# Moving the residual to the token layout: turned in place and sent in 32 transfers, in place of 160

## The chip, the core and the metric

The kernel runs on one core of a Trainium2 chip. The metric is device time in microseconds for one execution: the median of several runs. Five engines work side by side, each on an instruction queue of its own that it takes strictly in order: TensorE (PE, the matrix products), VectorE (DVE), ScalarE (ACT), GpSimd (POOL) and SyncE (SP). SP computes nothing; in this kernel it issues nearly all transfers (DMAs), which 16 DMA engines then carry out.

## What is computed

One decoder layer on 256 tokens of width 2048, with 16 meta tokens put ahead of them. Cut to what matters:

```python
h = concat(meta, x)                              # 272 tokens x 2048
...                                              # sparse attention and causal pooling
mix = concat(attn_out, pool_out) @ w_o
h = layer_norm(ALPHA * h + mix, ln1_g, ln1_b)
f = conv_gated_ffn(h, w_up, conv_w, conv_b, w_down)   # up to 2 x 5632, causal conv of width 3, gelu(a) * g, down
h = layer_norm(ALPHA * h + f, ln2_g, ln2_b)
return h[:, N_META:]
```

The change touches the term ALPHA * h of the last sum, the residual of the feed-forward part.

## The kernel before, in words

All matrix products are float32 work done in three passes: each operand is split into a high part and a low part (tiles with a middle dimension of 2), and high x high, high x low and low x high are added in PSUM. So every weight tile goes the same way. SP loads 1 MB into a raw tile (`wraw`, line 87), ACT writes the high half in two pieces (line 90), DVE subtracts and writes the low half in two pieces (line 91, tile `whl`), and TensorE uses it. There are three `wraw` and three `whl` buffers. `weights()` asks for the tile two ahead of the one in use, so SP's queue holds the loads in the order of use, each waiting for a `wraw` buffer to come free, and whatever else SP issues stands between them.

Up to the first layer norm the data lie with channels on the partitions: `y` is [128 partitions, 16 blocks of 128 channels, 272 tokens]. `normalise` (lines 629 to 637) finishes the first layer norm block by block in `y` and writes the split copy `hp` that the feed-forward part multiplies. The feed-forward part runs over 44 blocks f of 128 hidden channels, in four parts of 16, 12, 12 and 4 (`PARTS`). Each f takes two weight tiles (the two halves of `w_up`), 96 matmuls, two convolutions (`conv`, lines 660 to 662: one ACT and two DVE instructions each) and a gate (lines 677 to 681). For f below 4 (`FOLDED`) the normalisation is folded into the product, so that TensorE can start before `normalise` is done; from f = 4 on the products use `hp`. After the blocks of a part come the down products of that part, in four column groups c of 512 output channels, and line 735 adds each result to `y2`.

`y2` is [128 tokens, 2 token halves, 2048 channels]: here tokens lie on the partitions. The normalised h, which the residual needs, lies in `y` with channels on the partitions. So it has to be moved to the other layout before line 735 adds the first down product to it. That is done in two steps:

- `turn_blocks(m)` (lines 641 to 644) has DVE transpose block m in squares of 32 x 32, after the gates of f = 4 to 7, four blocks each. Each block is written one place further down: block m into the place of block m - 1, and block 0 into a spare tile of the ring (`blocks`, shown as `turned` in the trace). Each DVE instruction covers 128 x 256 elements.
- `residual(c, a, b, i)` (lines 646 to 654) has SP send squares to their places: for source partitions 32a to 32a + 31 and 32 tokens, the squares of the four blocks of one column group c go to the 32 partitions of those tokens. For c = 1 to 3 that is one transfer of 16 KB (line 651). For c = 0 it is two, 12 KB from `y` (line 653) and 4 KB from the spare tile (line 654). Every contiguous piece is 32 elements, or 128 bytes. In all that makes 128 moves and 160 transfers.

The moves are listed by column group first (line 656). After the gate of each f from 5 on, ten of them are issued (lines 716 to 718), and ten more in each column group of the down products of part 0 (lines 731 and 732), until none is left. So line 735 of column group c waits only for the transfers of that group.

The kernel is written in a tile framework. It places the semaphores and lays out each engine's queue when the program is built. It follows the order of the source roughly, but may put an instruction that is ready by its own estimate ahead of one that is not. It spreads the transfers of a queue over a fixed set of semaphores, so an issue can also have to wait until an earlier transfer has landed.

Of the kernel before, what the change touches and what calls it, by code (L numbers as in the profile page):

```python
# [11 lines left out]
F32 = mybir.dt.float32  # L12
# [5 lines left out]
P = 128  # L18
D = 2048
NM = 16  # L20
S = 256
T = NM + S
# [13 lines left out]
FOLDED = 4  # L36
# [14 lines left out]
def tile_layer(ctx, tc, xt, w_first, w_proj, w_uk, w_uv, w_pool, w_o, w_up, w_down, cols, rows, rel_bias, onehot, out):  # L51
    nc = tc.nc
    sb = ctx.enter_context(tc.tile_pool(name="sb", bufs=1))
    wp = ctx.enter_context(tc.tile_pool(name="wp", bufs=3))
    ring = ctx.enter_context(tc.tile_pool(name="ring", bufs=24))
# [4 lines left out]
    def big():  # L60
        return pm.tile([P, 512], F32, tag="mm", name="mm")
# [34 lines left out]
    def emit(i):  # L96
        if i in ready:
            return
        if i == last:

            raw = wp.tile([P, 2048], F32, tag="wraw", name="wraw")
            nc.sync.dma_start(raw, stream[i])
            ready[i] = []
            for c in range(0, 2048, 256):
                hl = ring.tile([P, 2, 256], F32R, tag="act", name="whl_r", padded_shape=[P, 2, T])
                nc.scalar.activation(hl[:, 0, :], raw[:, c:c + 256], AF.Copy)
                nc.vector.tensor_tensor(hl[:, 1, :], raw[:, c:c + 256], hl[:, 0, :].bitcast(F32), op=ALU.subtract)
                ready[i].append(hl)
            return
        if i == spare:  # L110
            raw = wp.tile([P, 2048], F32, tag="wraw", name="wraw")
            hl = sb.tile([P, 2, 2048], F32R, tag="y", name="whl_y")
        else:
            raw, hl = weight_tiles()
        fetch(raw, hl, stream[i], slice(0, 2048))
        ready[i] = hl
# [6 lines left out]
    def weights(ahead=2):  # L123
        i = state["use"]
        state["use"] += 1
        prefetch(i + 1 + ahead)
        return ready.pop(i)
# [7 lines left out]
    def product(ps, hl, m, act, lo, hi, ks=range(KT), width=P, k0=0, k1=KT):  # L135

        for n in range(k0, k1):
            k = ks[n]
            wh, wl = hl[:, 0, k * width:k * width + m], hl[:, 1, k * width:k * width + m]
            ah, al = act[k][:, 0, lo:hi], act[k][:, 1, lo:hi]  # L140
            nc.tensor.matmul(ps, wh, ah, start=n == 0, stop=False)  # L141
            nc.tensor.matmul(ps, wh, al, start=False, stop=False)  # L142
            nc.tensor.matmul(ps, wl, ah, start=False, stop=n == KT - 1)  # L143
# [3 lines left out]
    for k0, k1 in [(k, k + 1) for k in range(9)] + [(9, 12), (12, 15), (15, 16)]:  # L147
# [7 lines left out]
        for k in range(k0, k1):  # L155
            xk, wk, c = raw[:, k % 3, :T], raw[:, k % 3, T:], slice(k % 6 * MF, k % 6 * MF + MF)
            a = ring.tile([P, 2, T], F32R, tag="act", name="xp")
# [184 lines left out]
    y = sb.tile([P, KT, T], F32, tag="y", name="x", padded_shape=[P, KT, T])  # L342
# [26 lines left out]
    src = score  # L369
    for r in range(TOPK // 8):  # L370
# [4 lines left out]
        src = work  # L375
# [228 lines left out]
    def deviation():  # L604
        ps = small()
        column_sums([s1], cuts, 0, ps)
        column_sums([s2], cuts, 1, ps)
        for i, (a, b) in enumerate(cuts):
            r = slice(0, b - a)
            nc.vector.tensor_scalar_mul(st[r, 0, i:i + 1], ps[r, 64 * i:64 * i + 1], 1.0 / D)  # L610
            nc.vector.tensor_scalar(st[r, 1, i:i + 1], ps[r, 64 * (3 + i):64 * (3 + i) + 1], 1.0 / D, EPS,
                                    op0=ALU.mult, op1=ALU.add)
        nc.vector.tensor_tensor(st[:, 2, :], st[:, 0, :], st[:, 0, :], op=ALU.mult)
        nc.vector.tensor_tensor(st[:, 1, :2], st[:, 1, :2], st[:, 2, :2], op=ALU.subtract)
        nc.vector.tensor_tensor(st[:2, 1, 2:], st[:2, 1, 2:], st[:2, 2, 2:], op=ALU.subtract)
        nc.gpsimd.tensor_tensor(st[:, 2, :], st[:, 1, :], half, op=ALU.pow)
        nc.vector.scalar_tensor_tensor(st[:, 3, :], st[:, 0, :], -1.0, st[:, 2, :], op0=ALU.mult, op1=ALU.mult)

    def deviation_rows():
        for j, dst in ((2, rs), (3, m2)):  # L620
            ps = small()
            spread(st[:, j, :], cuts, ps)
            nc.scalar.activation(dst, ps[:, :NQ], AF.Copy)


    y2 = fp.tile([P, 2, D], F32, name="y2", bufs=1)
# [9 lines left out]
        nc.vector.tensor_tensor(a[:, 1, :NQ], yd, a[:, 0, :NQ].bitcast(F32), op=ALU.subtract)  # L636
        h_parts.append(a)

    blocks = ring.tile([P, 2, T], F32, tag="act", name="turned0")

    def turn_blocks(m):

        dst = y[:, m - 1, NM:] if m else blocks[:, 0, NM:]
        nc.vector.transpose(dst, y[:, m, NM:])

    def residual(c, a, b, i):

        src, dst, t = slice(32 * a, 32 * a + 32), slice(32 * b, 32 * b + 32), NM + i * P + 32 * b
        to = y2[dst, i, 512 * c:512 * c + 512].rearrange("p (m d) -> p m d", d=P)[:, :, src]
        if c:  # L650
            nc.sync.dma_start(to, y[src, 4 * c - 1:4 * c + 3, t:t + 32])
        else:
            nc.sync.dma_start(to[:, 1:], y[src, :3, t:t + 32])
            nc.sync.dma_start(to[:, 0], blocks[src, 0, t:t + 32])  # L654

    moves = [(c, a, b, i) for c in range(4) for a in range(4) for b in range(4) for i in range(2)]

    def conv(j, half_, src):
        z = fp.tile([P, S], F32, name="z", tag=f"z{half_}")
# [16 lines left out]
    def gate(za, zg):  # L676
        nc.scalar.activation(za, za, AF.Gelu_apprx_tanh)
        nc.vector.tensor_tensor(za, za, zg, op=ALU.mult)
        a = fp.tile([P, 2, S], F32R, name="gp", tag="gp", bufs=18, padded_shape=[P, 2, NE])
        nc.scalar.activation(a[:, 0, :], za, AF.Copy)  # L680
        nc.vector.tensor_tensor(a[:, 1, :], za, a[:, 0, :].bitcast(F32), op=ALU.subtract)
        return a
# [3 lines left out]
    for part, n in enumerate(PARTS):  # L686
        gated = []
        for f in range(f0, f0 + n):
            if part == len(PARTS) - 1 and f - f0 in (0, 2):
                emit((last, spare)[(f - f0) // 2])  # L690
            both = []
            for half_ in range(2):
                hl = weights()
                ps = big()
                if f < FOLDED:
                    k = 0
                    if f + half_ == 0:
                        product(ps[:, :NE], hl, P, folded, 0, NE, k1=7)
                        deviation()
                        product(ps[:, :NE], hl, P, folded, 0, NE, k0=7, k1=14)  # L700
                        deviation_rows()
                        k = 14
                    product(ps[:, :NE], hl, P, folded, 0, NE, k0=k)
                    while len(h_parts) < min(KT, 3 * (2 * f + half_ + 1)):
                        normalise(len(h_parts))
                    both.append(ps)
                else:
                    product(ps[:, :NQ], hl, P, h_parts, 0, NQ)
                    both.append(conv(half_ * FT + f, half_, ps))
            if f < FOLDED:  # L710
                both = [conv(half_ * FT + f, half_, unfold(both[half_])) for half_ in range(2)]
            gated.append(gate(*both))
            if FOLDED <= f < FOLDED + 4:
                for m in range(4):
                    turn_blocks(4 * (f - FOLDED) + m)
            if FOLDED + 1 <= f:
                for _ in range(min(10, len(moves))):
                    residual(*moves.pop(0))
        if part + 1 < len(PARTS):
            for c in range(4):  # L720
                ps = [big(), big()]
                for g in range(n // 4):
                    hl = weights()
                    for k in range(4 * g, 4 * g + 4):
                        w = slice(512 * (k - 4 * g), 512 * (k - 4 * g) + 512)
                        for i in range(2):
                            t = slice(i * P, (i + 1) * P)
                            nc.tensor.matmul(ps[i], gated[k][:, 0, t], hl[:, 0, w], start=k == 0, stop=False)  # L728
                            nc.tensor.matmul(ps[i], gated[k][:, 0, t], hl[:, 1, w], start=False, stop=False)  # L729
                            nc.tensor.matmul(ps[i], gated[k][:, 1, t], hl[:, 0, w], start=False, stop=k == n - 1)  # L730
                for _ in range(min(10, len(moves))):
                    residual(*moves.pop(0))
                for i in range(2):
                    yc = y2[:, i, 512 * c:512 * c + 512]
                    nc.vector.scalar_tensor_tensor(yc, yc, 1.0 if part else ALPHA, ps[i], op0=ALU.mult, op1=ALU.add)
        f0 += n
# [3 lines left out]
    for r in range(2):  # L740
        for c in range(4):
            t = fp.tile([P, 512], F32, name="gb", tag="gp", bufs=18, padded_shape=[P, 2 * NE])
# [5 lines left out]
    for i in range(2):  # L748
        t = slice(i * P, (i + 1) * P)
# [97 lines left out]
```

## Time and profile before

| | us |
|---|---|
| median of 3 runs | 1087.61 |
| lowest and highest of them | 1085.92, 1089.14 |
| the profiled execution | 1085.53 |
| its span, first to last instruction | 1083.7 |
| mean granted clock of TensorE in it | 0.995 |

The profiled execution lies 2.1 us below the median and 0.4 us below the lowest of the runs; its span is 1.8 us shorter than its time. Lines of the profile are quoted word for word. In a row for a line of the source, "L651 SPq" is an issue by SP's queue at line 651 of the kernel, and "x96" the number of instructions. "PEld" is TensorE's loading of the stationary operand, beside the matmuls. In rows of a table of stretches the numbers are the stretch, its length, then busy time (and instructions) of PE, PEld, DVE, ACT and POOL, then TensorE's granted clock, the mean busy share of the 16 DMA engines and what they moved in GB/s. In lists in order of time each row starts with start and length in us, and a bracket at its end gives the idle time before it and what ended it. "A <- B: 2.4, 1, 2.4" in a list of waits is the total in us, the number of times and the longest.

### The profile page before, as it was taken

The page shows a single profiled execution, that of the slowest core. Times are in us where ns is not written, and L with a number is a line of the kernel's source. Part 1 is how long each engine was busy: PE and PEld are TensorE (multiplying, and loading weights), DVE is VectorE, ACT ScalarE, POOL GpSimd, SP SyncE. Part 2 cuts the span into 40 slices and gives each one's busy share as a digit, 9 for nine tenths or more (in the row PEclk, how much of TensorE's full clock was granted, in tenths as well). Part 3 has the DMA queues.
Part 4 walks back from the last instruction along what each step waited for, and adds up shares of the span by engine and source line. Part 5 has one row for each costly group of instructions (what it writes and reads, how often), then busy time and mean ns, then how long its engine had stood idle before and what let it go on. Part 6 is the DMA issues. An engine that isn't in the chain of part 4 may idle for free.

```text
span 1083.7 us, 18829 instructions
## 1 busy us (share of the span) xinstructions
PE 1065.2 (98%) x7770; PEld 1009.2 (93%) x7770; DVE 713.4 (66%) x1083; ACT 525.3 (48%) x828; POOL 100.0 (9%) x131
## 2 busy tenths in 40 slices
PE   9999999999999998999999999999999999999995
PEld 8998999999999998999888999998899999988995
DVE  6879468849779974665445566665556666555757
ACT  6566456636458653454333445443344454434530
POOL 1100024126353200000000000000000000001000
PEclk9999999999999999999999999999999999999998
DMA  9755543444544555667655555555565555557712
GB/s 312 253 183 214 195 137 127 166 163 171 184 145 145 172 166 170 221 200 243 207 189 194 183 174 188 187 169 192 190 214 173 179 193 177 181 191 246 272 43 78
DMA packets 49702, 200.19 MB, mean 185 GB/s; under 512 B 22438, under 2 KB 22864, under 8 KB 27216
## 3 DMA queue, kind: packets, MB, share of 16 engines
q1 hardware_dynamic: 47920, 194.12, 52.3%
q0 software_dynamic: 1120, 3.82, 1.2%
q8 instruction: 61, 1.00, 0.4%
q10 hardware_dynamic: 576, 1.05, 0.3%
q14 instruction: 25, 0.20, 0.0%
HBM read 194.75 MB, written 2.11 MB: 182 GB/s over the span
## 4 chain that ended last, share of the span: by engine, by line
PE 91%; DVE 4%; DMA 3%; SPq 1%; ACT 1%; issue 1%; POOL 0%; ACTq 0%; DVEq 0%; POOLq 0%
PE mm L142 21%; PE mm L143 21%; PE mm L141 21%; PE mm L728 7%; PE mm L729 7%; PE mm L730 7%; DMA wraw<-in_w_up 1%; DVE whl L91 1%; DMA wraw<-in_w_first 1%; DVE x L632 1%; DVE hp L636 0%; DMA wraw<-in_w_proj 0%; SPq L654 0%; ACT whl L90 0%; PE at L295 0%
## 5 line engine op out<-in xcount | busy, mean ns | idle before, releaser
L91 DVE TENSOR_TENSOR whl<-wraw,whl 128x1024 fp32r<-128x1024 f32 x344 | 420.4, 1249 | 149.7 <-ACT whl L90 148.4
L90 ACT ACTIVATE whl<-wraw 128x1024 fp32r<-128x1024 f32 x344 | 346.9, 1050 | 197.3 <-PE mm L730 115.1
L141 PE MATMUL mm<-hp,whl 128*128 128x258 f32 x1280 | 364.1, 284 | 2.4 <-ACT whl L90 2.4
L142 PE MATMUL mm<-hp,whl 128*128 128x258 f32 x1280 | 363.6, 284 | 0.0
L143 PE MATMUL mm<-hp,whl 128*128 128x258 f32 x1280 | 361.9, 283 | 0.8 <-DVE whl L91 0.8
L143 PEld LDWEIGHTS mm<-hp,whl 128*128 128x128 f32 x1280 | 244.8, 191 | 1.0 <-DVE whl L91 1.0
L141 PEld LDWEIGHTS mm<-hp,whl 128*128 128x128 f32 x1280 | 242.4, 189 | 2.8 <-ACT whl L90 2.6
L142 PEld LDWEIGHTS mm<-hp,whl 128*128 128x128 f32 x1280 | 244.6, 191 | 0.1
L660 ACT ACTIVATE z<-mm,cv 128x256 f32<-128x256 f32 x80 | 44.9, 562 | 169.1 <-PE mm L143 169.1
L728 PE MATMUL mm<-whl,gp 128*128 128x512 f32 x320 | 126.3, 395 | 0.0
L661 DVE SCALAR_TENSOR_TENSOR z<-mm,cv,z 128x256 f32<-128x256 f32 x80 | 38.6, 482 | 133.2 <-ACT z L660 133.2
L730 PE MATMUL mm<-whl,gp 128*128 128x512 f32 x320 | 126.2, 394 | 0.0
L729 PE MATMUL mm<-whl,gp 128*128 128x512 f32 x320 | 126.1, 394 | 0.0
L141 PE MATMUL mm<-xp,whl 128*128 128x256 f32 (+5 forms) x384 | 110.9, 289 | 0.0
L143 PE MATMUL mm<-xp,whl 128*128 128x256 f32 (+5 forms) x384 | 109.0, 284 | 0.6 <-DVE whl L91 0.6
L142 PE MATMUL mm<-xp,whl 128*128 128x256 f32 (+5 forms) x384 | 109.5, 285 | 0.0
L730 PEld LDWEIGHTS mm<-whl,gp 128*128 128x128 f32 x320 | 60.1, 188 | 14.4
L143 PEld LDWEIGHTS mm<-xp,whl 128*128 128x128 f32 x384 | 72.4, 189 | 1.1 <-DVE whl L91 1.0
L728 PEld LDWEIGHTS mm<-whl,gp 128*128 128x128 f32 x320 | 60.2, 188 | 14.0
L141 PEld LDWEIGHTS mm<-xp,whl 128*128 128x128 f32 x384 | 72.7, 189 | 0.6
L729 PEld LDWEIGHTS mm<-whl,gp 128*128 128x128 f32 x320 | 60.1, 188 | 13.9
L142 PEld LDWEIGHTS mm<-xp,whl 128*128 128x128 f32 x384 | 72.3, 188 | 0.8 <-issue 0.5
(267 smaller groups left out, 1394.5 us busy)
## 6 DMA issues: line engine op xcount, KB each, us to landing
wraw<-in_w_up SPq DMA_DIRECT2D x88, 1024.0 KB, 4.9
wraw<-in_w_down SPq DMA_DIRECT2D x44, 1024.0 KB, 5.0
wraw<-in_w_proj SPq DMA_DIRECT2D x24, 1024.0 KB, 5.0
wraw<-in_w_o SPq DMA_DIRECT2D x16, 1024.0 KB, 4.9
wraw<-in_w_first SPq DMA_DIRECT2D x9, 304.0 KB, 5.9
x<-in_xt SPq DMA_DIRECT2D x1, 2176.0 KB, 8.3
gb<-in_rows POOLq DMA_DIRECT2D x8, 256.0 KB, 6.6
wraw<-in_w_first SPq DMA_DIRECT2D x2, 912.0 KB, 6.3
```

The source lines that it names most:

```text
L90: nc.scalar.activation(hl[:, 0, c], raw[:, c], AF.Copy)
L91: nc.vector.tensor_tensor(hl[:, 1, c], raw[:, c], hl[:, 0, c].bitcast(F32), op=ALU.subtract)
L141: nc.tensor.matmul(ps, wh, ah, start=n == 0, stop=False)
L142: nc.tensor.matmul(ps, wh, al, start=False, stop=False)
L143: nc.tensor.matmul(ps, wl, ah, start=False, stop=n == KT - 1)
L632: nc.vector.tensor_tensor(yd, yd, m2, op=ALU.add)
L660: nc.scalar.activation(z, src[:, 2:NQ], AF.Identity, bias=col(C_B, j), scale=col(C_W, 3 * j + 2))
L661: nc.vector.scalar_tensor_tensor(z, src[:, 1:NQ - 1], col(C_W, 3 * j + 1), z, op0=ALU.mult, op1=ALU.add)
L728: nc.tensor.matmul(ps[i], gated[k][:, 0, t], hl[:, 0, w], start=k == 0, stop=False)
L729: nc.tensor.matmul(ps[i], gated[k][:, 0, t], hl[:, 1, w], start=False, stop=False)
L730: nc.tensor.matmul(ps[i], gated[k][:, 1, t], hl[:, 0, w], start=False, stop=k == n - 1)
```

## The change

The spare tile and `turn_blocks` go. DVE turns each of the 16 blocks in its own place, at the same points of the source as before. Since all blocks then lie in one row, one transfer takes the squares of all 16 blocks for one pair of partition and token groups: `residual(a, b, i)` moves 32 partitions x 16 blocks x 32 elements, 64 KB in pieces of 128 bytes, and there are 32 of them. They are issued four at a time after the gates of f = 8 to 15, none in the down products. Each writes to all four column groups of `y2`.

```diff
-    blocks = ring.tile([P, 2, T], F32, tag="act", name="turned0")
-
-    def turn_blocks(m):
-
-        dst = y[:, m - 1, NM:] if m else blocks[:, 0, NM:]
-        nc.vector.transpose(dst, y[:, m, NM:])
-
-    def residual(c, a, b, i):
+    def residual(a, b, i):
 
         src, dst, t = slice(32 * a, 32 * a + 32), slice(32 * b, 32 * b + 32), NM + i * P + 32 * b
-        to = y2[dst, i, 512 * c:512 * c + 512].rearrange("p (m d) -> p m d", d=P)[:, :, src]
-        if c:
-            nc.sync.dma_start(to, y[src, 4 * c - 1:4 * c + 3, t:t + 32])
-        else:
-            nc.sync.dma_start(to[:, 1:], y[src, :3, t:t + 32])
-            nc.sync.dma_start(to[:, 0], blocks[src, 0, t:t + 32])
-
-    moves = [(c, a, b, i) for c in range(4) for a in range(4) for b in range(4) for i in range(2)]
+        to = y2[dst, i, :].rearrange("p (m d) -> p m d", d=P)[:, :, src]
+        nc.sync.dma_start(to, y[src, :, t:t + 32])
+
+    moves = [(a, b, i) for a in range(4) for b in range(4) for i in range(2)]
...
             if FOLDED <= f < FOLDED + 4:
-                for m in range(4):
-                    turn_blocks(4 * (f - FOLDED) + m)
-            if FOLDED + 1 <= f:
-                for _ in range(min(10, len(moves))):
+                for m in range(4 * (f - FOLDED), 4 * (f - FOLDED) + 4):
+                    nc.vector.transpose(y[:, m, NM:], y[:, m, NM:])
+            if FOLDED + 4 <= f and part == 0:
+                for _ in range(4):
                     residual(*moves.pop(0))
...
-                for _ in range(min(10, len(moves))):
-                    residual(*moves.pop(0))
```

## The prediction

> **What bounds the kernel now.** I read the page's first part, then the waits of TensorE, then its instructions in order of time around the one wait that matters, then a table of stretches.
>
> ```profile
> PE 1065.2 (98%) x7770; PEld 1009.2 (93%) x7770; DVE 713.4 (66%) x1083; ACT 525.3 (48%) x828; POOL 100.0 (9%) x131
> ```
>
> TensorE is busy for 98% of the span. The edit removes no matrix product, so it can win only where TensorE stands still because of the residual's transfers. Two views show what there is, first the waits of TensorE from 340 to 600 us (total, times, longest), then its instructions around them (start, us; idle time before in brackets):
>
> ```profile
> PE mm L141 <- ACT whl L90: 2.4, 1, 2.4
> PE mm L143 <- DVE whl L91: 1.5, 2, 0.8
> ```
>
> ```profile
> 416.82 0.28 PE L143 MATMUL mm<-hp,whl 128*128 128x258 f32 x1
> 419.54 0.39 PE L141 MATMUL mm<-hp,whl 128*128 128x258 f32 x1 [2.44 <-ACT whl L90]
> 419.76 0.28 PE L142 MATMUL mm<-hp,whl 128*128 128x258 f32 x1
> 420.80 0.58 PE L143 MATMUL mm<-hp,whl 128*128 128x258 f32 x1 [0.75 <-DVE whl L91]
> ...
> 424.08 0.28 PE L143 MATMUL mm<-hp,whl 128*128 128x258 f32 x1
> ```
>
> One hole, at 417 to 421 us, is all that TensorE loses while the residual is moved. The table of stretches (PE busy and matmuls, PEld, DVE, ACT, POOL, granted clock, DMA share, GB/s) gives the pace on either side:
>
> ```profile
> 345.00:394.00 49.00, 49.00 (x408) 48.97 (x407) 46.12 (x80) 33.79 (x56) 6.23 (x5) 1.00 0.52 174
> 404.00:414.00 10.00, 10.00 (x85) 10.00 (x84) 5.20 (x9) 2.83 (x5) 0.00 (x0) 1.00 0.08 13
> 420.00:424.00 4.00, 3.25 (x16) 3.20 (x16) 3.96 (x6) 3.65 (x6) 0.00 (x0) 0.57 0.25 42
> 425.00:485.00 60.00, 60.00 (x500) 60.00 (x499) 39.78 (x57) 31.05 (x43) 0.00 (x0) 1.00 0.69 227
> 640.00:700.00 60.00, 60.00 (x500) 60.00 (x499) 38.22 (x54) 29.67 (x43) 0.00 (x0) 1.00 0.54 183
> ```
>
> With transfers running (425 to 485) TensorE does 500 matmuls in 60 us, and without any (640 to 700) the same 500: 0.120 us each. So transfers cost nothing there, and everything is in the hole. I count it in matmuls: from the start at 416.82 to the start at 424.08 lie 18 of them (the omitted rows run L142, L143, L141 without a break) in 7.26 us, where 18 x 0.120 = 2.16 us would do. **The hole costs 5.1 us**: 2.44 + 0.75 = 3.2 us of waiting, and 1.9 us because the first matmuls behind it run at a granted clock of 0.57.
>
> What made the hole is read from the chain of waits between 405 and 425 us, and from SP's queue:
>
> ```profile
> 413.23 5.12 DMA wraw<-in_w_up
> ...
> 418.43 1.06 ACT whl L90
> ...
> 419.52 1.24 DVE whl L91
> ...
> 420.80 0.58 PE mm L143
> ```
>
> ```profile
> 394.62 1.77 SPq L87 DMA_DIRECT2D wraw<-in_w_up  x2
> ...
> 413.23 0.99 SPq L87 DMA_DIRECT2D wraw<-in_w_up  x2
> ```
>
> A pair of weight tiles left SP's queue at 394.62, the next at 413.23, 18.6 us later. Between them stood ten moves of column c = 0, two transfers each. TensorE eats a pair in 96 x 0.120 = 11.5 us. It still waited only 3.2 us, so **a gap of up to 18.6 - 3.2 = 15.4 us between pairs stays hidden** behind the three buffers, 3.9 us more than the pace; rather more, since the pairs before had stood behind transfers too and the buffers weren't full. That figure carries much of what follows.
>
> **The change part by part.** The durations of issues and of the turns (ns min/median/max, first and last start):
>
> ```profile
> L654 SPq DMA_DIRECT2D y<-turned x32: 507/595/1517, 356.1 to 416.3; - x32
> ```
>
> ```profile
> L653 SPq DMA_DIRECT2D y<-x x32: 585/605/672, 366.9 to 415.7; - x32
> ```
>
> ```profile
> L651 SPq DMA_DIRECT2D y<-x x96: 585/600/1485, 417.0 to 533.3; - x96
> ...
> DMA to landing us min/median/max: 1.8/4.5/8.4
> ```
>
> ```profile
> L644 DVE STREAM_TRANSPOSE x<-x x15: 425/436/447, 357.9 to 378.5; 128x256 f32<-128x256 f32 x15
> ```
>
> ```profile
> L735 DVE SCALAR_TENSOR_TENSOR y<-y,mm x24: 679/687/689, 524.9 to 1005.2; 128x512 f32<-128x512 f32 x24
> ```
>
> *Issues removed.* 160 issues of about 0.60 us are 96 us of SP's queue; 32 remain. An issue of 4 KB takes 595 ns, of 12 KB 605, of 16 KB 600: it doesn't follow the size. I take 0.6 us for 64 KB, with some 0.05 us between issues: 4 x 0.65 = 2.6 us for each f from 8 to 15, in which a pair is due every 11.5 us. From f = 5 to 7 nothing is moved, so the twenty transfers that stood ahead of the pair at 413.23 are gone, and the gap there falls back to what the buffers dictate. The lower end for an issue is 0.6 us. The upper, if it grew with the 512 pieces of 128 bytes instead of 128, is 4 x 0.6 = 2.4 us, or 9.6 us per f. That is what ten transfers take per f now between 425 and 485 us, where TensorE doesn't wait. Both ends give the same sum, and I take the lower, since the three rows are flat.
>
> *Bytes.* They stay: 32 x 512 = 16,384 pieces of 128 bytes. In the stretch 404 to 414 hardly anything but these moves: 13 GB/s for 10 us are 130 KB or some 1000 pieces, at a share of 0.08 x 16 engines x 10 us = 12.8 engine-us, so 12.8 ns a piece. A transfer of 64 KB thus holds each of 16 engines for 32 x 12.8 ns = 0.41 us. From above, 425 to 485 against 640 to 700: 0.15 x 16 x 60 = 144 engine-us more, for some 50 transfers of 128 pieces (96 in 116 us), 22.5 ns a piece and 0.72 us a transfer, although the weights also ran faster there. A pair of weights behind four new transfers comes 1.6 to 2.9 us later by the data and 2.6 by the issues, 5.5 at most. Between 425 and 485 us ten transfers stand between pairs, with over 9 us of issue (a row below), and TensorE keeps its pace. So I take nothing.
>
> *The turns.* Sixteen remain, each now onto its own block. A turn in place isn't in the trace; the nearest row, one block further, has 436 ns. I take that. Nothing speaks for less than 0.43 us; from above I allow double, 16 x 0.44 = 7 us more of DVE in the stretch 345 to 394, where DVE is busy for 46.12 of 49 us. That is 4.1 us more than the stretch holds. The cover is the tiles that are split ahead, with those 3.9 us or more, and DVE's empty time behind it (5.20 busy of 10 us); if the cover were gone, it would cost the 4.1 us. The spare ring tile that held block 0 goes; no row shows anyone waiting for it.
>
> *Waits that appear.* Every transfer now needs all sixteen turns, not four:
>
> ```profile
> SPq L653 <- DVE x L644: 2.9, 1, 2.9
> ...
> SPq L654 <- DMA wraw<-in_w_up: 2.5, 2, 2.3
> ```
>
> These are SP's own waits between 340 and 425 us. SP takes its queue in order, so weights stand behind a transfer that waits for a turn, and ACT, DVE and TensorE behind them. The last turn starts at 378.5 us; the first transfer is written after the gate of f = 8, which is past 400 us, so I count nothing. Were it planned where the first L653 stands now (366.9), it would hold the queue 378.9 - 366.9 = 12 us, still under 15.4. The second row, a transfer held until a weight tile has landed, belongs to the hole and goes with it.
>
> At the other end, the first addition into y2 (L735, column 0) must now wait for all 32 transfers. It starts at 524.9. The weights of f = 15 leave SP at 486.60:
>
> ```profile
> 486.60 1.01 SPq L87 DMA_DIRECT2D wraw<-in_w_down  x2
> 487.66 9.24 SPq L651 DMA_DIRECT2D y<-x  x10
> ```
>
> Four transfers behind them are issued by 487.66 + 2.6 = 490.3 and, with the longest landing seen (8.4) and 1.6 us for their larger size, in place by about 500: 25 us of cover.
>
> *Two rules beside the rows.* The granted clock of 0.57 after 2.44 + 0.75 us of waiting is the row. The Trainium skill (TensorE: Matmul & The Clock Gate, What's actually happening) says that the clock halves after an idle window of about 3.4 us. Taken strictly, this hole is too short for it and would be worth 3.2 us instead of 5.1; the trace shows it slowed all the same. The other rule is the first rival's.
>
> *The sum.* The profiled execution took 1085.53 us, span 1083.7 and 1.8 around it. 1085.5 - 5.1 = 1080.4. The median of the runs shown, 1087.6, is 2.1 above that execution; I see nothing in the edit that touches this difference, so the forecast is 1087.6 - 5.1 = **1082.5 us**.
>
> **The rivals.** *The weights were late through the data, not the issues (no change).* Then 16,384 pieces still block them, and the hole only moves: 1087.6. The Trainium skill (DMA: Bandwidth & Descriptors, Issuing engines are not separate DMA queues) speaks for it: the time to initiate a transfer is usually small beside the transfer. Against it stands the row 404 to 414: the DMA engines were 0.08 busy while SP issued one transfer after another, so here issue, 0.60 us against 0.10 us of data (8 pieces an engine), was the larger. Chance 0.16, with smaller remains of the hole.
>
> *All 32 are pulled together (slower).* The queue's order isn't the source's: in the source each L653 stands ahead of its L654, yet four L654 went first.
>
> ```profile
> 356.07 2.52 SPq L654 DMA_DIRECT2D y<-turned  x4
> ...
> 366.90 3.24 SPq L653 DMA_DIRECT2D y<-x  x5
> ```
>
> If the plan pulled all 32 into one gap behind the last turn, near 379 us, a pair would wait 32 x 0.65 = 20.8 us. TensorE would then wait 20.8 - 15.4 = 5.4 us, with 1.9 for the clock 7.3 against 5.1 now: 2.2 slower, 1089.8. It decides from 24 transfers in one gap (15.4 / 0.65). Against it: from 425 us on each pair is followed by just ten, although all were ready. Chance 0.12.
>
> *The turn in place isn't the same instruction's work*, needing a detour or a pass at double length whose 4.1 us come through: 1082.5 + 4.1 = 1086.6, among the first rival's times. I give it 0.03 of those 0.16.
>
> **How the numbers follow.** The forecast has 0.72, the no-change rival 0.16, the slower one 0.12. About 0.3%, or 3.3 us, is what a measurement can tell from no change: faster means below 1084.3. The forecast's own range is 1079.5 (the profiled sum, less a microsecond of spread) to 1084.3, whose top allows the hole to be worth only its 3.2 us of waiting. To leave out no more than 2 in 10, the range takes in the no-change case: 1079.5 to 1087.7. Faster 0.72, same 0.16, slower 0.12.
>
> **What would show it.** TensorE's waits from 340 to 600 us should keep no entry of 2.4 us and the granted clock should stay at 1.00; pairs of weights should be no more than 12 to 13 us apart; issues of 64 KB should take 0.6 us, turns 0.44; L735 should wait for TensorE, not for DMA. It is wrong if a new wait for whl appears between 380 and 500 us, or if an issue takes above (11.5 - 0.7) / 4 = 2.7 us, from which SP becomes the bound.

## The result, and the profile after

| | before | after |
|---|---|---|
| median of 6 runs each, us | 1086.63 | 1080.76 |
| lowest and highest, us | 1085.55, 1089.14 | 1079.81, 1084.16 |
| profiled execution, us | 1085.53 | 1081.53 |
| its span, us | 1083.7 | 1079.7 |
| mean granted clock of TensorE | 0.995 | 0.997 |

The ratio of the times is 0.9948, with a 95% interval of 0.993 to 0.9965: 3.8 to 7.6 us faster. The forecast was 1082.5 us in a range of 1079.5 to 1087.7, with 5.1 us of gain. With more runs, the median of the kernel before turned out 1.0 us lower than the one that the forecast started from.

The waits of TensorE from 335 to 600 us, and the table of the same stretches as in the prediction, both of the kernel after:

```profile
PE mm L143 <- DVE whl L91: 0.7, 1, 0.7
```

```profile
345.00:394.00 49.00, 48.95 (x407) 48.73 (x406) 47.02 (x82) 35.00 (x56) 7.05 (x6) 1.00 0.70 226
404.00:414.00 10.00, 10.00 (x86) 10.00 (x85) 5.65 (x9) 4.09 (x6) 0.00 (x0) 1.00 0.64 176
420.00:424.00 4.00, 4.00 (x36) 4.00 (x35) 3.10 (x5) 1.40 (x3) 0.00 (x0) 1.00 0.68 166
425.00:485.00 60.00, 60.00 (x500) 60.00 (x500) 38.18 (x54) 30.35 (x43) 0.00 (x0) 1.00 0.68 206
640.00:700.00 60.00, 60.00 (x500) 60.00 (x499) 36.74 (x52) 29.48 (x42) 0.00 (x0) 1.00 0.55 184
```

The waits of 2.44 and 0.75 us are gone, and with them the granted clock of 0.57: the row 420 to 424 now has 36 matmuls at a clock of 1.00, where there were 16. The 0.7 us that remain lie at 342 us, ahead of the residual, and were there before (the list of before had 1.5 in two waits, of which 0.75 belonged to the hole).

The spans differ by 4.0 us only, not 5.1. The difference is mostly in the start. Two landmarks show it, the first product on `hp` (f = 4) and the first down product of part 0 (the time before "to" is the first start). Before, then after:

```profile
L141 PE MATMUL mm<-hp,whl x1280: 277/284/420, 359.0 to 1049.7; 128*128 128x258 f32 x183
```

```profile
L728 PE MATMUL mm<-whl,gp x320: 387/394/404, 503.0 to 1003.0; 128*128 128x512 f32 x160
```

```profile
L141 PE MATMUL mm<-hp,whl x1280: 277/284/293, 360.4 to 1046.0; 128*128 128x258 f32 x183
```

```profile
L717 PE MATMUL mm<-whl,gp x320: 387/395/404, 499.3 to 999.3; 128*128 128x512 f32 x160
```

The profiled execution after reached f = 4 at 360.4, 1.4 us later than the one before, although nothing up to there was edited. 0.9 us of it were already there at the first weight of the projections, which SP issued at 17.8 us instead of 16.9, so it comes from the start. From there to the down products it took 138.9 us instead of 144.0, which is 5.1 us less, the size of the hole. Behind the stretch the new kernel gained another 0.3 us. I call this **the stretch** and use it below, since it leaves the spread of the start out; over all profiles here the first landmark lies between 358.2 and 360.4 us.

SP's queue after, where L643 is the residual's transfer:

```profile
374.42 1.41 SPq L643 DMA_DIRECT2D y<-x  x2
378.22 0.35 SPq L87 DMA_DIRECT2D wraw<-in_w_up  x1
378.62 1.27 SPq L643 DMA_DIRECT2D y<-x  x2
381.73 0.33 SPq L87 DMA_DIRECT2D wraw<-in_w_up  x1
...
463.40 0.59 SPq L643 DMA_DIRECT2D y<-x  x1
469.08 0.33 SPq L87 DMA_DIRECT2D wraw<-in_w_up  x1
469.45 1.26 SPq L643 DMA_DIRECT2D y<-x  x2
```

One or two transfers stand behind each weight tile, from 374 us on. The source puts four behind each second tile, and none before f = 8. The plan moved them up into idle time of the queue. Their issues and the turns:

```profile
L643 SPq DMA_DIRECT2D y<-x x32: 591/602/1610, 374.4 to 470.1; - x32
...
DMA to landing us min/median/max: 2.7/5.4/7.5
```

```profile
L704 DVE STREAM_TRANSPOSE x<-x x16: 396/430/435, 345.0 to 373.9; 128x256 f32<-128x256 f32 x16
```

```profile
L722 DVE SCALAR_TENSOR_TENSOR y<-y,mm x24: 682/689/690, 521.2 to 1001.4; 128x512 f32<-128x512 f32 x24
```

An issue of 64 KB takes 602 ns, as one of 4 KB did, and a turn in place 430 ns against 436. The last transfer is issued at 470 and lands within 8 us; the first addition into `y2` starts at 521.

### The profile page after: what moved, and what is told of

The parts are those of the page before. It is cut to its first block, busy times and chain, and to the rows that moved or that the text cites. A ratio compares the mean times of both kernels' runs of the same rounds, so it can differ in the third digit from the quotient of the medians.

```text
span 1079.7 us, 18694 instructions
## 1 busy us (share of the span) xinstructions
PE 1064.7 (99%) x7770; PEld 1008.5 (93%) x7770; DVE 712.5 (66%) x1083; ACT 524.9 (49%) x828; POOL 100.0 (9%) x131
## 4 chain that ended last, share of the span: by engine, by line
PE 92%; DVE 5%; DMA 2%; ACT 1%; issue 0%; POOL 0%; SPq 0%; ACTq 0%; DVEq 0%; POOLq 0%
PE mm L142 22%; PE mm L141 22%; PE mm L143 21%; PE mm L717 7%; PE mm L718 7%; PE mm L719 7%; DVE whl L91 1%; DMA wraw<-in_w_first 1%; DVE x L632 1%; DVE hp L636 1%; DMA wraw<-in_w_proj 1%; PE at L295 0%; PE mm L747 0%; PE mm L745 0%; PE at L296 0%
```

## Experiments

My theory: SP spends so long issuing the residual's transfers between two weight tiles that the weights come late. Rivals: the bytes delay the weights on the DMA engines; the number of issues in all is what costs; the gain comes from turning in place; the gain needs large transfers. The table has the stretch of each run from its profile, and the ratio of its time to that of the kernel before with the 95% interval. For runs that were executed once it has that one time, and the comparison rests on the stretch.

| run | first `hp` product to first down product | stretch, us | against before |
|---|---|---|---|
| before | 359.0 to 503.0 | 144.0 | |
| after | 360.4 to 499.3 | 138.9 | 0.9948 (0.993 to 0.9965) |
| e1, in place alone | 358.5 to 497.4 | 138.9 | 0.9949 (0.9931 to 0.9966) |
| e2, large transfers alone | 358.2 to 497.3 | 139.1 | 0.995 (0.9934 to 0.9965) |
| e3, slower pace alone | 358.3 to 497.4 | 139.1 | 0.9945 (0.993 to 0.996) |
| e4, GpSimd's queue | 359.9 to 500.4 | 140.5 | 0.9963 (0.9949 to 0.9976) |
| e5, order of the source | 360.0 to 498.9 | 138.9 | 0.9947 (0.9929 to 0.9966) |
| e6, 32 in one gap | 358.9 to 504.3 | 145.4 | 1.0014 (0.9999 to 1.0029) |
| e7, 20 in one gap | 358.7 to 504.4 | 145.7 | one run, 1086.84 us |
| e8, 20, queues of ACT and DVE set | 359.9 to 498.8 | 138.9 | one run, 1081.06 us |
| e9, 32, queues set | 358.8 to 500.3 | 141.5 | one run, 1083.28 us |
| e10, 4, queues set | 358.6 to 497.5 | 138.9 | one run, 1079.72 us |

**e1: in place, but 128 transfers of 16 KB**

```diff
-        dst = y[:, m - 1, NM:] if m else blocks[:, 0, NM:]
-        nc.vector.transpose(dst, y[:, m, NM:])
+        nc.vector.transpose(y[:, m, NM:], y[:, m, NM:])
...
-        if c:
-            nc.sync.dma_start(to, y[src, 4 * c - 1:4 * c + 3, t:t + 32])
-        else:
-            nc.sync.dma_start(to[:, 1:], y[src, :3, t:t + 32])
-            nc.sync.dma_start(to[:, 0], blocks[src, 0, t:t + 32])
+        nc.sync.dma_start(to, y[src, 4 * c:4 * c + 4, t:t + 32])
```

> One part of the change alone: the turns in place, but 128 transfers of 16 KB, ten per f from f = 5 as before. Issue theory (SP's time for issuing between two pairs of weights made the hole; above 15.4 us it shows): column 0 now needs one issue per move, at most about 6 x 0.65 = 3.9 us between two weight tiles, so no wait of 2.4 us in TensorE, granted clock 1.00, and 5 us less than before, as much as the whole change. Data theory (the bytes of column 0 at f = 5 to 7 delayed the weights): same bytes at the same time, the hole stays, 0 us. Size theory (it takes transfers of 64 KB): 0 us.

The stretch is 138.9 us, as with the whole change. So the large transfers aren't needed. The plan put four to six of these transfers behind each weight tile around the place of the old hole, so per pair of tiles about ten moves went out, as before, with half the issues: the same bytes between the weights, and no hole.

**e2: 32 transfers of 60 KB and 32 of 4 KB, blocks turned one place down as before**

```diff
-        to = y2[dst, i, 512 * c:512 * c + 512].rearrange("p (m d) -> p m d", d=P)[:, :, src]
+        to = y2[dst, i, :].rearrange("p (m d) -> p m d", d=P)[:, :, src]
...
+        nc.sync.dma_start(to[:, 1:], y[src, :KT - 1, t:t + 32])
+        nc.sync.dma_start(to[:, 0], blocks[src, 0, t:t + 32])
```

> The other part alone: each block still turned one place down, block 0 in the spare tile, but 32 transfers of 60 KB and 32 of 4 KB after the gates of f = 8 to 15. Issue theory: 64 issues, no more than about six between two weight tiles, no hole, 5 us less than before. If turning in place is what counts (fewer buffers or waits on DVE): hole or time as before, 0 us.

139.1 us. So turning in place isn't needed either. Each half of the change is enough alone, and nothing adds up, since there was only one hole to close.

**e3: the kernel before, with five moves after a gate instead of ten**

```diff
-                for _ in range(min(10, len(moves))):
+                for _ in range(min(5 if f < 11 else 14, len(moves))):
```

> The kernel before with nothing changed but the pace: five moves instead of ten after each gate of f = 5 to 10, fourteen from f = 11 on. Still 160 issues. Issue theory: ten issues of column 0 are 6.5 us between pairs of weights, under 15.4, so the hole goes and 5 us with it, without the change. If the total number of issues is what costs (160 x 0.6 us), or the small transfers as such: 0 us, or a hole elsewhere.

139.1 us, with all 160 issues, the spare tile and the small transfers as before. One number in the source brings the whole gain. SP's queue in this run, and the waits of TensorE from 335 to 620 us:

```profile
388.39 0.61 SPq L653 DMA_DIRECT2D y<-x  x1
389.04 0.59 SPq L654 DMA_DIRECT2D y<-turned  x1
389.73 0.53 SPq L87 DMA_DIRECT2D wraw<-in_w_up  x1
...
393.09 0.61 SPq L653 DMA_DIRECT2D y<-x  x1
393.79 0.53 SPq L87 DMA_DIRECT2D wraw<-in_w_up  x1
```

```profile
PE mm L143 <- DVE whl L91: 0.7, 1, 0.7
```

The issues still take 0.6 us each, but four to six now stand between two weight tiles. In the kernel before, f = 5 to 7 asked for twenty issues and two weight loads each: 20 x 0.65 + 0.7 = 13.7 us of SP's queue for 11.5 us of TensorE's work. By this count it fell behind by 2.2 us with each f, and further where an issue waited for a landing. Of the 18.6 us ahead of the pair at 413.23, this count explains 13.7. In the other 4.9 SP waited 2.3 us for a weight tile to land (the longest wait of L654 in the prediction's list) and 0.9 us on DVE, and single issues took up to 1.5 us. Together they are the hole; whether the count alone would have made one is not shown. The total of 160 isn't the cause. This run can't tell issues from bytes, since it spreads out both.

**e4: all 160 issues on GpSimd's queue**

```diff
-            nc.sync.dma_start(to, y[src, 4 * c - 1:4 * c + 3, t:t + 32])
+            nc.gpsimd.dma_start(to, y[src, 4 * c - 1:4 * c + 3, t:t + 32])
```

and the same for the two transfers of column 0.

> The kernel before with all 160 transfers issued from GpSimd's queue instead of SP's, same sizes, same points of the source. Issue theory: SP's queue holds weights only, no hole, 5 us less than before. Data theory: the bytes still meet the weights on the same 16 engines, the hole stays, 0 us. Risk for either: an issue on GpSimd may take longer, which would show as a wait of the first addition into y2 for DMA.

140.5 us: the old hole is gone, although the same bytes went out earlier (the last transfer of line 651 at 467 us instead of 533). So the bytes on the shared DMA engines weren't its cause. But 1.6 us are lost elsewhere. The expectation of the full 5 us failed. A row of its stretches, two of the waits from 345 to 385 us, and the chain of waits up to TensorE's late start show where:

```profile
375.00:385.00 10.00, 8.95 (x72) 8.54 (x71) 9.86 (x19) 6.66 (x11) 8.61 (x17) 1.00 0.55 182
```

```profile
ACT z L660 <- POOL u L673: 5.0, 3, 2.2
...
PE mm L143 <- DVE whl L91: 1.0, 1, 1.0
```

```profile
371.71 0.52 POOL y L653
...
372.24 0.77 POOL u L673
...
373.03 0.61 ACT z L660
...
377.79 1.14 DVE whl L91
...
378.98 0.39 PE mm L143
```

GpSimd still has additions to do for f below 4 (`u`, line 673), and its queue now has issues of 0.51 to 0.55 us between them. ACT's convolutions wait for these additions, 5.0 us in all against 3.1 in the kernel before, and TensorE waits 1.0 us for a split that stands behind. The chain links the two: the last addition ends 13.1 us after the first product on `hp`, where it was 11.3 in the kernel before, and convolutions, turns, a gate and the split stand behind it on the chain. No run moves the additions alone.

**e5: the changed kernel with SP's queue forced into the order of the source**

```diff
-        nc.sync.dma_start(raw[:, c], src)
+        d = nc.sync.dma_start(raw[:, c], src)
+        if state.get("pin"):
+            tc.keep_in_program_order(d)
...
-        nc.sync.dma_start(to, y[src, :, t:t + 32])
+        tc.keep_in_program_order(nc.sync.dma_start(to, y[src, :, t:t + 32]))
```

with `state["pin"]` set for f = 4 to 15 and the down products behind them.

> The changed kernel with SP's queue forced into the order of the source for part 0: pair of weights, four transfers of 64 KB, pair of weights, and so on from f = 8 to 15, as the prediction had assumed (the changed kernel has one or two behind each weight tile, from 374 us on). Issue theory: 2.6 us of issue between pairs, far under 15.4, time as the changed kernel, 5 to 6 us less than before. If the even spreading is what helped: a wait for whl between 400 and 500 us and 1 us or more lost.

138.9 us. The even spreading that the plan chose isn't needed.

**e6 and e7: 32 or 20 transfers in one gap.** As e5, with the number of moves after the gate of f = 8 raised:

```diff
-                for _ in range(4):
+                for _ in range(min(len(moves), 32 if f == FOLDED + 4 else 4)):
```

> The changed kernel with SP's queue forced so that all 32 transfers stand between two pairs of weights at f = 8: 32 x 0.65 = 20.8 us. The prediction's slower rival and its limit of 15.4 us: TensorE waits 5.4 us and loses 1.9 by the clock, 2.2 us slower than before, 7.3 slower than the changed kernel. If the limit is higher with full buffers (three raw and three split tiles, up to about 20 us): a wait of 0 to 2 us and a time near the changed kernel's. If issues don't matter at all: time of the changed kernel.

> As the run with 32 in one gap, but 20 there and four in each of the next three: 20 x 0.65 = 13 us between two pairs. By the limit of 15.4 us no wait in TensorE and the time of the changed kernel. If 20 issues in one gap make the hole whatever stands around them: 3 us of wait as in the kernel before.

145.4 and 145.7 us. The slower rival's size came out nearly as forecast (1.4 us over before in the stretch, 2.2 forecast), but its reason didn't: 20 transfers cost as much as 32, and TensorE waits 3.5 us in both. In e7 the two weight tiles behind the block are issued at 413.97 and 414.6 and land 5.6 and 8.4 us later, by 423.0, while TensorE's wait begins near 428. The list in order of time for ACT, TensorE's first matmul behind the wait and a row of the stretches, all of e7 (here ACT's split is line 92, the convolution's first step line 651, the gate's last line 671):

```profile
428.36 0.56 ACT L651 ACTIVATE z<-mm,cv 128x256 f32<-128x256 f32 x1 [3.67 <-PE mm L145]
430.45 0.42 ACT L671 ACTIVATE gp<-z 128x256 fp32r<-128x256 f32 x1 [1.53 <-DVE z L669]
430.77 3.88 ACT L92 ACTIVATE whl<-wraw 128x1024 fp32r<-128x1024 f32 x4
```

```profile
431.87 0.58 PE L143 MATMUL mm<-hp,whl 128*128 128x258 f32 x1 [3.55 <-ACT whl L92]
```

```profile
432.00:436.00 4.00, 3.54 (x15) 3.24 (x16) 4.00 (x4) 2.65 (x3) 0.00 (x0) 0.50 0.27 33
```

ACT was idle for 3.67 us, waiting for TensorE to finish the block in work. The split that TensorE needed next stood behind that convolution and its gate on ACT's queue. The plan had put it there, presumably because it took the weights to be late. So the wait is the way from the end of one product over convolution, gate and split to the next, whatever the weights did. From 428.04 to 437.76 us TensorE started 24 matmuls in 9.72 us where 24 x 0.120 = 2.88 would do: 6.8 us lost, 4.0 of them in this wait and a second of 0.46, the rest at a clock of 0.50. e8 to e10 test this reading.

**e8, e9, e10: the same blocks of 20, 32 and 4, with splits, convolutions and gates kept in the order of the source**

```diff
-            nc.scalar.activation(hl[:, 0, c], raw[:, c], AF.Copy)
+            pin(nc.scalar.activation(hl[:, 0, c], raw[:, c], AF.Copy))
...
+    def pin(ins):
+        return tc.keep_in_program_order(ins) if state.get("own") else ins
```

and `pin` around the split's subtraction and the three steps of the convolution, for f = 8 to 15 and the down products behind them. The gates follow by their operands.

> The changed kernel with 20 transfers between two pairs of weights, as in the run before, but with the splits, convolutions and gates of f = 8 to 15 forced to stand on ACT's and DVE's queues in the order of the source, so that a split is never queued behind the gate of the block in work. In the run with 20 the stretch from the first product on hp to the first down product took 145.7 us, in the changed kernel 138.9. Queue-order theory (the wait of 3.5 us there came from a split that the plan had put behind a gate, not from late weights): 138.9 here. Limit theory (a gap of 15.9 us is over the 15.4): about 0.5 us of wait and a slowed clock, 139.5 to 141.5. If 20 transfers delay the weights by themselves: 145.7.

> The same with all 32 transfers between two pairs: 24.0 us from pair to pair. Limit of 15.4 us: 8.6 us of wait and 1.9 by the clock, 149.4 for the stretch. If full buffers hide about 22 to 24 us: 0 to 3 us of wait and 139 to 144.

> The control: the same forced queues of ACT, DVE and SP with four transfers after each pair. 138.9 for the stretch if forcing the order costs nothing by itself.

With 20 transfers in one gap the stretch is 138.9 us and there is no wait: the 6.8 us that e7 lost came from the order of the splits, convolutions and gates and not from the transfers. The trace of e7 shows that order on ACT's queue; DVE's was set along with it and not apart. The control has 138.9 as well. With 32, the weights are late: ACT and TensorE of e9, and a row of its stretches:

```profile
428.63 2.00 ACT L92 ACTIVATE whl<-wraw 128x1024 fp32r<-128x1024 f32 x2 [9.19 <-DMA wraw<-in_w_up]
```

```profile
429.74 0.39 PE L146 MATMUL mm<-hp,whl 128*128 128x258 f32 x1 [1.28 <-ACT whl L92]
431.00 0.39 PE L148 MATMUL mm<-hp,whl 128*128 128x258 f32 x1 [0.75 <-DVE whl L93]
```

```profile
420.00:440.00 20.00, 17.97 (x147) 17.55 (x146) 9.09 (x12) 8.48 (x12) 0.00 (x0) 1.00 0.84 281
```

Now ACT waits for DMA, as in the kernel before. SP's queue shows the gap that caused it:

```profile
398.60 23.77 SPq L648 DMA_DIRECT2D y<-x  x32
422.48 1.52 SPq L87 DMA_DIRECT2D wraw<-in_w_up  x3
```

From the last weight issue, at 398.06, to the next at 422.48 are 24.4 us. TensorE waited 1.28 + 0.75 = 2.0 us. With full buffers some 22 us stay hidden, not 15.4.

## Why the prediction was right, point by point

- *Only the hole is at stake, and it costs 5.1 us.* Right. The stretch is shorter by 5.1 us, and no other wait of TensorE changed between 340 and 600 us. Counting matmuls across the hole gave the size, where the waits alone would have given 3.2.
- *SP's issues made it, not the bytes.* Right, and shown two ways: e4 with the same bytes from another queue, e1 with the same bytes in half the issues of column 0. e3, with the same issues spread out, shows that their pace is what counts. The no-change rival falls. The rule that it leant on (the Trainium skill, DMA: Bandwidth & Descriptors, Issuing engines are not separate DMA queues), that the time to initiate a transfer is usually small beside the transfer, doesn't decide here. Against the 0.10 to 0.18 us for which a transfer of 16 KB held each DMA engine by the prediction's two readings, its issue of 0.60 us was the larger; against the 4.5 us from issue to landing it was small. But SP's issues stood one behind the other, while the transfers overlapped. And part of what held SP was waiting for landings (2.3 us in one gap), which the prediction counted to the hole without a price of its own.
- *An issue of 64 KB takes 0.6 us.* Right: 602 ns at the median.
- *A new transfer holds each DMA engine for 0.41 to 0.72 us.* Right. From 425 to 485 us 13 were issued, and the DMA share rose from 0.55 (640 to 700) to 0.68. So each held each DMA engine for 0.13 x 60 / 13 = 0.60 us, inside the range. It is an upper figure, since the weights also ran a little faster there: 206 - 184 = 22 GB/s more, of which 13 transfers of 64 KB in 60 us are 14. It is hidden either way.
- *A turn in place takes as long as one to the next block.* Right: 430 against 436 ns. DVE was busy for 47.02 of 49 us in its fullest stretch, and TensorE didn't wait there.
- *The transfers are issued behind the gates of f = 8 to 15, past 400 us.* Wrong in place, without effect. They went out from 374 to 470 us, one or two behind each weight tile. Ahead of the first, SP waited for the last turn (its waits from 340 to 480 us in the kernel after):

```profile
SPq L643 <- DVE x L704: 1.7, 1, 1.7
```

  I had allowed for such a hold (12 us, still hidden). e5 shows that the assumed order gives the same time.
- *A gap of up to 15.4 us stays hidden.* Too low, as the prediction suspected. It was read at a place where the queue was behind already: SP took 23.2 us for three weight tiles, from 371.38 to 394.62, which TensorE uses in 17.3. With full buffers it is 22 us (e9).
- *The slower rival.* It didn't happen, since the plan spreads transfers that are ready. Forced (e6), it costs 1.5 us more than before by the ratio, though the interval (-0.1 to 3.1) still holds no difference. That is near the 2.2 forecast by luck: of the 6.5 us that its stretch is over the changed kernel's, 3.9 go when the order on ACT's and DVE's queues is set (e9). With that order set, the stretch is still 2.5 us shorter than before.
- *1082.5 us.* 1.7 us above the 1080.8 measured. In the profiled executions the edit gave the 5.1 us of the sum. Of the 1.7, 1.0 is the base: it was the median of three runs, 1087.6, and that of six is 1086.6. The other 0.8 is the gain between the medians, 5.9 instead of 5.1, with 3.8 to 7.6 around it by the ratio's interval. The hole was measured in one execution; the 19 runs of the kernel before beside e5 spread from 1082.0 to 1090.9 us, so 5.1 need not be its size in each.

## What to carry to other kernels

Add up what an issuing queue has to do between two of its urgent transfers (here 20 x 0.65 + 0.7 us against 11.5 us of matmuls), not over the whole kernel: 160 issues cost nothing once ten instead of twenty stood in the critical blocks. One such gap is not the trouble either: twenty issues between two pairs cost nothing with full buffers (e8). They cost time in the kernel before, where the queue was already behind. Before rebuilding a data path to have fewer transfers, try a slower pace for those there are: that was one number here. And when a wait doesn't change with the amount of work that is thought to cause it (20 or 32 transfers), look at what stands ahead on the waiting engine's own queue.

## What was not expected of the hardware and the plan

The granted clock fell after some waits of TensorE and not after others: in the kernel before it was 0.57 (row 420 to 424) after waits of 2.44 and 0.75 us, in e7 it was 0.50 (row 432 to 436) after 3.55 and 0.46, and it stayed at 1.00 (row 420 to 440 of e9) after 1.28 and 0.75. Where between these the limit lies, and whether single waits or their sum decide, no run here shows. The Trainium skill (TensorE: Matmul & The Clock Gate, What's actually happening) puts the fall at an idle window of about 3.4 us; the hole of the kernel before had no single wait that long. At the median an issue on SP's queue takes 0.33 us for a weight tile of 1 MB and 0.60 us for a transfer of 4 to 64 KB in pieces of 128 bytes, whatever the size. The plan's order reaches further than the queue that was edited: with the loads held up on SP's queue, splits stood behind gates on ACT's, and setting the order won 6.8 us back (e7 against e8).
